# TensorE in program order through three attention pipelines, their side work placed anew

## The chip, the cores and the metric

The kernel runs on one core of a Trainium2 chip. The metric is the time of one launch in microseconds (us) of device time. The kernel before was run three times: 1625.69 to 1627.4 us, median 1627.03 us.

A core has five engines with a queue each: TensorE (PE in the profile, its weight loads PEld), VectorE (DVE), ScalarE (ACT), GpSimd (POOL) and SyncE (SP, which here only starts DMA transfers). TensorE writes its products to PSUM, which has eight banks of 512 f32 columns in 128 partitions.

## The reference, cut to what matters

The model has two blocks. Block 1 has a pooling mixer and a layer of stick-breaking attention; block 2 has latent attention and differential attention, each with modulation (shift, scale, gate) from a vector.

```python
# block 1, layer 1: stick-breaking attention, 16 heads of 64, 512 tokens
logits = q @ k.T * scale                       # strictly causal
a = sigmoid(logits) * prod(sigmoid(-logits) over the later keys)
x = x + (a @ v * silu(z)) @ w_out              # z: gate, a projection of h

# block 2: modulation of each layer, for c and for c_ctx
shift, scale, gate = split(silu(c) @ ada_w[i] + ada_b[i], 3)   # ada_w[i]: 1024 x 3072
h = x * (1 + scale) + shift                    # h_c from the context likewise

# layer 0: latent attention, 16 heads, 512 tokens + 256 of context
q = rope(rms(h W_qa) W_qb);  k, v = rms(h W_kva) W_kvb
o = softmax(q k^T) v * silu(gate)

# layer 1: differential attention, 8 heads, two maps each
o = softmax(q1 k1^T) v - lam * softmax(q2 k2^T) v
o = rms_norm(o) * g_sub * silu(gate)
x = layer_norm(ALPHA * x + gate * (o @ out_w))
```

## The kernel before, in words

Everything is float32. A projection is taken as three products of float32r parts (`mm3`, L147 to L149: high times high, high times low, low times high). Weights come in units of 512 KB through `wraw` (three buffers in SBUF): SP loads them, ACT takes the high part (`wh`, L126), POOL the low part (`wl`, L127).

PSUM is divided into four parts: `lg` (two tiles of two banks, logits), `tr` (two banks, used in turn by all transposes), `pv` (one bank, products of probabilities and values) and `mm` (one bank, for the projections that run inside a pipeline).

Each of the three attentions is a `pipeline` of steps (L238). A step has a first half (logits and what follows on ACT, DVE and POOL) and a second half, emitted `lag` steps later (transposes of the probabilities, products with the values). Into each step *pieces* are emitted: projections for later heads, gates, and the modulation vectors. A piece has a group (a step that needs the group calls `need`, which emits what is left of it) and a due step; in the kernel before, every piece that is due comes between the first and the second half.

- The stick pipeline has 24 steps (8 pairs of heads, three steps each), lag 2. The preparation of a pair transposes its keys and queries into two banks of `tr` (`kT_p`, `qT_p`) and copies them out as high and low parts: keys on ACT and DVE (`K`, L663, L664), queries on ACT (`Q`, L670, L671) and DVE (`QL`, L672). The second half transposes the weights (`aT_p`), copies them out (L713, L715) and multiplies with the values (L725).
- The latent pipeline has 80 steps (16 heads, four blocks of queries and one of the context each), lag 2. The queries of a head are transposed (`qT_p`) and copied out by ACT (L1012) and DVE (L1013). The probabilities are transposed (`PT_p`); after two heads their products with the values go to the one bank of `pv` (L1056), first for the 512 tokens (`PT`), then for the context (`PTc`), and each is multiplied out of the bank by DVE (L1057).
- The differential pipeline has 32 steps (8 heads, four blocks of queries each), lag 1. The preparation of a head (`prep`) transposes queries and keys: `q_p` (four transposes, one bank of `tr`) and `k_p` (four for the first 512 tokens, one bank, and two for the rest, the other bank), in this order, two maps each copied by ACT (L1376, L1377, L1385) and DVE (L1378, L1386). The last second half of a head ends with the products (`pv`, L1418), a norm on ACT and DVE (L1422, L1423, L182 to L187, L1426), four transposes of the normalised output (`o_p`) and their product with the gate (L1431).

The modulation of a layer is a product of a vector pair with 1024 x 3072 weights. `ada_piece` (L755 on) loads one block of 128 rows (`araw`, L764, in a buffer of `wraw`) and adds two products of 32 columns (L767) to a bank of `pv`; eight pieces make one third. The four column groups of 32 of the array hold two halves of the sum and two halves of the columns, so up to four products can run side by side.

What the kernel writes is not the order in which the engines run. The framework's scheduler reorders the instructions of each engine by its own estimates; only what is wrapped in `keep_in_program_order` keeps its place.

Of the kernel before, what the change touches and what calls it, by code (L numbers as in the profile page):

```python
# [19 lines left out]
P = 128  # L20
# [9 lines left out]
FREE = 10 ** 6  # L30
GRID_W = 64
# [10 lines left out]
class Block:  # L42
    def __init__(self, ctx, tc, a, out):
        self.ctx, self.tc, self.nc, self.a, self.out = ctx, tc, tc.nc, a, out
        self.nc.scalar.preload_act_table_set("natural_log_exp_and_others")
        self.st = ""
        self.last_pair = None
# [97 lines left out]
    def mm3(self, out, lh, ll, rh, rl, start, stop):  # L145
        mm = self.nc.tensor.matmul
# [31 lines left out]
    def rsqrt(self, ss, n, scale):  # L178
        """(ss * scale + eps)^-1/2 on a small tile."""
# [25 lines left out]
    def silu_mul(self, out, sg, z):  # L205
        """out = z * sigmoid(z), sg: a tile for the sigmoid."""
# [3 lines left out]
    def split(self, x, pool, tag, gain=None, n=512, bufs=8):  # L210
        """x * gain as the exact sum of two float32r parts."""
# [11 lines left out]
    def row_bcast(self, out, cols):  # L223
        """cols [128 tok, blocks] -> out [128, tok]: the value of each token in every partition."""
        for t in range(cols.shape[1]):
            self.nc.tensor.matmul(out[:, t * P:(t + 1) * P], lhsT=cols[:, t:t + 1].to_broadcast([P, P]), rhs=self.ident, start=True, stop=True)

    def token_ss(self, acc, n, name):
        """acc [128, tok]: sums over partitions, one column for each block of 128 tokens."""
        pr = self.p_tr(name)  # L230
        for t in range(n):
            self.nc.tensor.matmul(pr[:, t:t + 1], lhsT=acc[:, t * P:(t + 1) * P], rhs=self.ones[:, :1], start=True, stop=True)
# [22 lines left out]
    def need(self, group):  # L255
        while any(p[0] <= group for p in self.pieces):
            i = next(i for i, p in enumerate(self.pieces) if p[0] != FREE)
            self.pieces.pop(i)[1]()

# [45 lines left out]
    def pT(self, i, pool):  # L305
        """p[i]^T in two float32r parts."""
# [24 lines left out]
    def ple(self, acts, pT, xT, pool, done, step=None):  # L331
        """x += (p @ ple_w) * sigmoid(x @ ple_gate_w); done(c) follows on each chunk."""
# [164 lines left out]
    def head_norm(self, pp, tb0, dst, pool):  # L497
        """pp [128, 2 blocks, 4 heads x 64] -> dst[:, tb0:tb0+2], each head at unit rms of the normalised input."""
# [27 lines left out]
    def layer1(self):  # L526
# [7 lines left out]
        # k, q and later the outputs of two pairs of heads in each slab  # L534
# [109 lines left out]
    def stick_steps(self, c, ks, qs, vtok, ogs, pool):  # L644
        """Stick-breaking attention of heads 2c and 2c+1: with keep = sigmoid(-l), the weight of key s is
        sigmoid(l_s) times the product of keep over the later keys."""
# [5 lines left out]
        def prep():  # L652
            # [qh; qh], ql and [kh; kl] of each head: two passes carry all three products
# [21 lines left out]
        def first(n, segs):  # L675
# [4 lines left out]
            for e, i, o in segs:  # L680
                w = (i + 1) * P
                s, qi = half[e], slice(i * P, (i + 1) * P)
                nc.tensor.matmul(L[:, o:o + w], lhsT=Q[e][:, qi], rhs=K[e][:, :w], start=True, stop=False)
                nc.tensor.matmul(L[:, o:o + w], lhsT=QL[s, qi], rhs=K[e][s, :w], start=False, stop=False)
                nc.tensor.matmul(L[:, o + i * P:o + w], lhsT=self.identb, rhs=self.maskb, start=False, stop=True)
            kp = pool.tile([P, 1024], F32, tag="sb_k", name="sb_k", bufs=2)
            bt = h["bt", n] = pool.tile([P, 1024], F32, tag="sb_b", name="sb_b", bufs=4)
# [7 lines left out]
            # the last key of a block is masked: its weight is zero as it stands  # L695
# [5 lines left out]
        def second(n, segs):  # L701
# [19 lines left out]
            for j in range(NT):  # L721
                for e in range(2):
                    hd = 2 * c + e
                    av = aT[e][:, 4 * j:10 + j:3, :]
                    nc.tensor.matmul(pv[64 * e:64 * e + 64, j * P:], lhsT=vtok[j][:, hd * 64:(hd + 1) * 64], rhs=av, start=(j == 0), stop=(j == NT - 1))  # L725
# [10 lines left out]
    def ada_setup(self):  # L736
# [9 lines left out]
        # rows 32 * (2 * half of the sum + half of the columns) + vector are summed to 2 * half of the columns + vector  # L746
# [6 lines left out]
    def ada_pieces(self, q, steps):  # L753
        """Shift, scale or gate of a layer (q = 3 * layer + part): one piece for each block of 128 rows."""
        return [(FREE, lambda k=k: self.ada_piece(q, k), n) for k, n in enumerate(steps)]  # L755

    def ada_piece(self, q, k):
        nc = self.nc
        layer, part = divmod(q, 3)
        if k == 0:  # L760
            self.ada_ps = self.p_pv("ada_p")
        ps = self.ada_ps
        raw = self.wp.tile([P, 1024], F32, tag="wraw", name="araw", bufs=3)
        nc.sync.dma_start(out=raw, in_=self.a["ada_w_2"][layer, k * P:(k + 1) * P, part * 1024:(part + 1) * 1024])  # L764
        for b in range(2):
            j = 2 * (k % 2) + b
            nc.tensor.matmul(ps[32 * j:32 * j + 32, :], lhsT=self.cs[:, k, :], rhs=raw[:, b * 512:(b + 1) * 512], start=(k < 2), stop=(k >= 6), tile_position=(0, 32 * j))  # L767
        if k < 7:
            return
        row = self.wp.tile([P, 1024], F32R, tag="wh", name="ada_row", bufs=4).bitcast(F32)  # L770
        nc.vector.tensor_copy(out=row[:, :512], in_=ps)
# [725 lines left out]
```

## Time and profile before

| | |
|---|---|
| runs, median (lowest to highest) | 1627.03 us (1625.69 to 1627.4) |
| profiled execution, span | 1627.5 us |
| PE busy | 1558.4 us, 96% of the span |
| PEld, DVE, ACT, POOL busy | 1260.5, 927.2, 714.9, 601.7 us |
| the three pipelines in the trace | stick 386 to 553 us, latent 779 to 1060 us, differential 1212 to 1573 us |

PE is busy for nearly all of the span. A busy time counts the modelled ends of pipelined matmuls, so it can hide short waits; how far one start lies behind the next says more. A plain f32 matmul (transposes, `ada_p`, `pv` of the latent pipeline) leaves two records where it is done in two passes: for `ada_p` and `pv` the count in a row is twice that of the program's matmuls.

### The profile page before, as it was taken

The numbers are of one execution on the slowest core, as the hardware profiler recorded it, in microseconds if no ns is written. First come the engines' busy times: TensorE is split into PE (matmuls) and PEld (weight loads), VectorE is DVE, ScalarE is ACT, GpSimd is POOL, SyncE is SP. The second block draws the span as 40 slices with busy tenths as digits, with TensorE's granted clock in tenths as the row PEclk, the third lists the DMA queues.
The fourth block names the chain that finished last, engine by engine and source line by source line (L and its number), as shares of the span: only waits on it lengthen the run. The fifth ranks groups of instructions, "written<-read, shape, count | busy, mean of one in ns | idle before, by whom it ended". The sixth has DMA issues, their size and how long they took to land.

```text
span 1627.5 us, 24398 instructions
## 1 busy us (share of the span) xinstructions
PE 1558.4 (96%) x9590; PEld 1260.5 (77%) x9590; DVE 927.2 (57%) x1769; ACT 714.9 (44%) x1315; POOL 601.7 (37%) x431
## 2 busy tenths in 40 slices
PE   6999999999999999999999999997899999999997
PEld 4777889997655688888766666596888888898887
DVE  6676465524766656242655666558855544545566
ACT  5323354436555333332755555623334443544542
POOL 2433555553444453212323332443433323243310
PEclk9999999999999999999999999997997999999999
DMA  5323432322334344311103122254231101121112
GB/s 159 88 78 91 123 117 77 100 92 79 109 124 133 114 133 108 83 46 43 40 2 119 46 71 78 66 182 149 83 96 40 39 27 39 40 66 40 53 64 106
DMA packets 149748, 136.01 MB, mean 84 GB/s; under 512 B 12613, under 2 KB 135225, under 8 KB 149633
## 3 DMA queue, kind: packets, MB, share of 16 engines
q1 hardware_dynamic: 149632, 134.45, 26.6%
q8 instruction: 76, 1.25, 0.3%
q14 instruction: 40, 0.32, 0.1%
HBM read 126.02 MB, written 8.40 MB: 83 GB/s over the span
## 4 chain that ended last, share of the span: by engine, by line
PE 47%; DVE 4%; issue 2%; DMA 2%; ACT 1%; POOL 1%; SPq 0%; DVEq 0%; POOLq 0%; ACTq 0%
PE PT_p L172 5%; PE pv L1056 4%; PE qkv_p L147 3%; PE qkv_p L149 3%; PE qkv_p L148 3%; PE lg L1399 3%; PE pv L1418 3%; PE lg L1398 2%; PE gt_p L147 2%; PE gt_p L148 2%; PE gt_p L149 2%; PE lg L147 2%; PE lg L148 2%; PE lg L149 2%; PE ada_p L767 1%
## 5 line engine op out<-in xcount | busy, mean ns | idle before, releaser
L127 POOL TENSOR_TENSOR wl<-wraw,wh 128x1024 fp32r<-128x1024 f32 (+2 forms) x159 | 376.7, 2379 | 381.2 <-ACT wh L126 362.6
L126 ACT CAST wh<-wraw 128x1024 fp32r<-128x1024 f32 (+2 forms) x164 | 166.6, 1020 | 287.7 <-issue 61.1
L1073 ACT ACTIVATE pe<-lg,st 128x768 f32<-128x768 f32 x160 | 130.4, 816 | 99.3 <-DVE st L1072 76.7
L1072 DVE TENSOR_REDUCE st<-lg 128x1 f32<-128x768 f32 x160 | 134.5, 846 | 47.1 <-PE lg L1399 28.3
L1035 POOL TENSOR_SCALAR pe<-pe,st 128x768 f32<-128x768 f32 (+1 forms) x96 | 73.3, 764 | 159.7 <-DVE st L1074 154.5
L147 PE MATMUL qkv_p<-wh,h 128*128 128x256 f32 x384 | 110.6, 288 | 0.3 <-ACT V L1345 0.2
L149 PE MATMUL qkv_p<-wh,h 128*128 128x256 f32 x384 | 108.9, 284 | 0.2 <-DVE h L217 0.2
L148 PE MATMUL qkv_p<-wl,h 128*128 128x256 f32 x384 | 108.8, 284 | 0.0
L172 PEld LDWEIGHTS PT_p<-ident,pe 128*128 128x128 f32 x640 | 71.6, 142 | 43.5 <-POOL pe L1035 15.9
L172 PE MATMUL PT_p<-ident,pe 128*128 128x128 f32 x640 | 99.3, 280 | 4.4 <-POOL pe L1035 1.4
L1403 POOL TENSOR_SCALAR pe<-pe,st 128x768 f32<-128x768 f32 x32 | 29.1, 909 | 148.1 <-DVE st L1402 96.8
L147 PEld LDWEIGHTS qkv_p<-wh,h 128*128 128x128 f32 x384 | 73.5, 191 | 2.3 <-DVE st L1072 0.5
L147 PE MATMUL out_p<-wh,o 128*128 128x256 f32 x256 | 74.1, 290 | 0.9 <-DVE y L1271 0.8
L148 PE MATMUL out_p<-wl,o 128*128 128x256 f32 x256 | 73.4, 288 | 1.4 <-POOL wl L127 1.4
L147 PE MATMUL kv_p<-wh,kv 128*128 128x256 f32 x256 | 72.7, 284 | 1.3 <-ACT kv L219 1.2
L148 PEld LDWEIGHTS qkv_p<-wl,h 128*128 128x128 f32 x384 | 73.5, 191 | 0.5 <-issue 0.2
L149 PEld LDWEIGHTS qkv_p<-wh,h 128*128 128x128 f32 x384 | 73.2, 191 | 0.8 <-DVE h L217 0.4
L149 PE MATMUL out_p<-wh,o 128*128 128x256 f32 x256 | 73.3, 290 | 0.1
L148 PE MATMUL kv_p<-wl,kv 128*128 128x256 f32 x256 | 72.1, 282 | 0.0
L149 PE MATMUL kv_p<-wh,kv 128*128 128x256 f32 x256 | 71.7, 282 | 0.0
L697 POOL TENSOR_TENSOR sb_b<-sb_b,sb_k 128x1023 f32<-128x1023 f32 (+1 forms) x32 | 43.2, 1360 | 74.3 <-DVE sb_k L694 51.0
L694 DVE TENSOR_TENSOR_SCAN sb_k<-sb_k 128x512 f32<-128x512 f32 (+3 forms) x64 | 56.8, 933 | 6.8 <-ACT sb_k L689 6.5
(453 smaller groups left out, 4574.0 us busy)
## 6 DMA issues: line engine op xcount, KB each, us to landing
araw<-in_ada_w_dram SPq DMA_DIRECT2D x48, 512.0 KB
wraw<-in_diff_w_in_dram SPq DMA_DIRECT2D x32, 512.0 KB
wraw<-in_out_w_dram SPq DMA_DIRECT2D x24, 512.0 KB
wraw<-in_a_w_in_dram SPq DMA_DIRECT2D x16, 512.0 KB
wraw<-in_ple_gate_w_dram SPq DMA_DIRECT2D x16, 512.0 KB
wraw<-in_w_kv_dram SPq DMA_DIRECT2D x16, 512.0 KB
wraw<-in_b_w_in_dram SPq DMA_DIRECT2D x16, 512.0 KB
wraw<-in_mla_w_in_dram SPq DMA_DIRECT2D x11, 512.0 KB
```

The lines of the kernel that those rows point to most:

```text
L126: nc.scalar.copy(h[:, :n], raw[:, :n])
L127: (nc.vector if i < 3 or pool == "ow3" else nc.gpsimd).tensor_tensor(out=l[:, :n], in0=raw[:, :n], in1=h[:, :n].bitcast(F32), op=ALU.subtract)
L147: mm(out, lhsT=lh, rhs=rh, start=start, stop=False)
L148: mm(out, lhsT=lh, rhs=rl, start=False, stop=False)
L149: mm(out, lhsT=ll, rhs=rh, start=False, stop=stop)
L172: self.nc.tensor.transpose(out, in_, self.ident[:in_.shape[0], :in_.shape[0]])
L694: nc.vector.tensor_tensor_scan(out=kp[:, rev], data0=kp[:, rev], data1=kp[:, rev], initial=1.0, op0=ALU.mult, op1=ALU.min)
L1035: nc.gpsimd.tensor_scalar(out=pe, in0=pe, scalar1=st[:, 1:2], scalar2=0.0, op0=ALU.mult, op1=ALU.add)
L1056: nc.tensor.matmul(pv[64 * ee:64 * ee + 64, :], lhsT=V[:, k0 + k, vs], rhs=HH[px][:, k, :], start=(k == 0), stop=(k == nk - 1))
L1072: nc.vector.tensor_reduce(out=st[:, 0:1], in_=L, axis=AX.X, op=ALU.max, negate=True)
L1073: nc.scalar.activation(pe, L, AF.Exp, bias=st[:, 0:1], accum_out=st[:, 2:3])
L1399: nc.tensor.matmul(L[:, cs], lhsT=QL[s, qs], rhs=K[m][s, cs], start=False, stop=True)
```

## The change

1. Inside `pipeline` a flag is set, and while it is set every matmul and transpose is wrapped in `keep_in_program_order`: TensorE then runs them as the program emits them. The other engines are scheduled as before.
2. After a step's first half one due piece is emitted, the other due ones after the second half. `need` leaves modulation pieces and their loads where they are.
3. A modulation piece takes two blocks of rows, loaded by a piece of their own one step earlier; its four products go side by side to the `mm` bank, each complete in itself, and DVE adds them up in an SBUF tile (`arow`). Before, the sum over eight pieces stayed in a bank of `pv`.
4. The pieces of the stick and the latent pipeline get other due steps; those of the differential pipeline keep theirs. One tile of the stick pipeline (`sb_b`) has three buffers where it had four.

```diff
+    def pe(self, ins):
+        return self.tc.keep_in_program_order(ins) if self.in_order else ins
+
+    def mm(self, *args, **kw):
+        return self.pe(self.nc.tensor.matmul(*args, **kw))
+
     def transpose(self, out, in_):
-        self.nc.tensor.transpose(out, in_, self.ident[:in_.shape[0], :in_.shape[0]])
+        self.pe(self.nc.tensor.transpose(out, in_, self.ident[:in_.shape[0], :in_.shape[0]]))
...
         self.mm_banks("mm")
+        self.in_order = True
         for n in range(len(steps) + lag):
             if n < len(steps):
                 steps[n][0]()
-            while pieces and pieces[0][2] <= n:
-                self.piece()
+            self.due(n, 1)
             if n >= lag:
                 steps[n - lag][1]()
-
-    def piece(self):
-        self.pieces.pop(0)[1]()
+            self.due(n, len(pieces))
+        self.in_order = False
+
+    def due(self, n, most):
+        while self.pieces and self.pieces[0][2] <= n and most:
+            p = self.pieces.pop(0)
+            p[1]()
+            most -= p[0] != LOAD
...
-            n = 6 * q + 3
-            pieces += self.ada_pieces(q, [n + k // 2 for k in range(8)])
+            n = 6 * q + 4
+            pieces += self.ada_pieces(q, [n, n + 1, n + 3, n + 4])
...
+    def ada_load(self, q, k):
+        layer, part = divmod(q, 3)
+        raws = self.araw[q, k] = []
+        for i in (2 * k, 2 * k + 1):
+            raws.append(self.wp.tile([P, 1024], F32, tag="wraw", name="araw", bufs=3))
+            self.nc.sync.dma_start(out=raws[-1], in_=self.a["ada_w_2"][layer, i * P:(i + 1) * P, part * 1024:(part + 1) * 1024])
...
-            self.ada_ps = self.p_pv("ada_p")
-        ps = self.ada_ps
-        raw = self.wp.tile([P, 1024], F32, tag="wraw", name="araw", bufs=3)
-        nc.sync.dma_start(out=raw, in_=self.a["ada_w_2"][layer, k * P:(k + 1) * P, part * 1024:(part + 1) * 1024])
-        for b in range(2):
-            j = 2 * (k % 2) + b
-            nc.tensor.matmul(ps[32 * j:32 * j + 32, :], lhsT=self.cs[:, k, :], rhs=raw[:, b * 512:(b + 1) * 512], start=(k < 2), stop=(k >= 6), tile_position=(0, 32 * j))
+            self.arow = self.pools["mla1" if layer else "att"].tile([P, 512], F32, tag="arow", name="arow", bufs=1)
+        row = self.arow
+        ps = self.p_mm("ada_p")
+        for i, raw in enumerate(self.araw.pop((q, k))):
+            for b in range(2):
+                j = 2 * i + b
+                self.mm(ps[32 * j:32 * j + 32, :], lhsT=self.cs[:, 2 * k + i, :], rhs=raw[:, b * 512:(b + 1) * 512], start=True, stop=True, tile_position=(0, 32 * j))
+        if k == 0:
+            nc.vector.tensor_copy(out=row, in_=ps)
+        else:
+            nc.vector.tensor_tensor(out=row, in0=ps, in1=row, op=ALU.add)
...
-            pieces += K(2 * g + 1, n + 2, n + 3)
+            pieces += K(2 * g + 1, n + 1, n + 3)
             if g < 3:
-                pieces += V(g + 1, [n + 6, n + 7, n + 9]) + K(2 * g + 2, n + 10, n + 11) + Q(g + 1, [n + 12, n + 13, n + 14, n + 14, n + 15, n + 16])
+                pieces += K(2 * g + 2, n + 10, n + 11) + Q(g + 1, [n + 12, n + 13, n + 14, n + 14, n + 15, n + 15]) + V(g + 1, [n + 17, n + 18, n + 19])
         for q in range(3, 6):
-            pieces += self.ada_pieces(q, [20 * q - 38 + k for k in range(8)])
+            n = 20 * q - 60
+            pieces += self.ada_pieces(q, [n + 5, n + 7, n + 8, n + 9])
```

The set of TensorE's instructions is the same in both kernels; their order is not. Three places follow, in the order in which TensorE has them.

The end of a head in the differential pipeline, before the change. `qkv_p` is a projection for a later head, `o_p` the transposes behind the norm, `lg` the logits of the next step; the head's last `pv` stands 48 `qkv_p` matmuls ahead of `o_p`:

```order
L147 MATMUL qkv_p<-wh,h_10632 128x256
L148 MATMUL qkv_p<-wl,h_10632 128x256
L149 MATMUL qkv_p<-wh,h_10632 128x256
L172 MATMUL o_p<-ident,on_11751 128x128 x4
L1398 MATMUL lg_11771<-K,Q 128x256
L1399 MATMUL lg_11771<-K,QL 128x256
```

The same place after the change:

```order
L179 MATMUL qkv_p<-wl,h_10668 128x256
L179 MATMUL qkv_p<-wh,h_10668 128x256
L182 MATMUL PT_p<-ident,pe 128x128 x6
L179 MATMUL pv_11762<-V_10789,AT 128x128 x24
L182 MATMUL o_p<-ident,on_11787 128x128 x4
L179 MATMUL lg_11807<-K,Q 128x512
```

The transposes `o_p` now follow the head's last products directly, in seven of the eight heads; in the eighth, products of the out projection stand between.

The preparation of a head in the differential pipeline, before the change, at the last two of the six key transposes (`k_p`); the first four stand 49 rows further up, and `gt_p` is the projection of a gate:

```order
L147 MATMUL gt_p<-h_10730,wh 128x256
L148 MATMUL gt_p<-h_10730,wh 128x256
L149 MATMUL gt_p<-h_10730,wl 128x256
L172 MATMUL k_p<-ident,kr 128x128 x2
L172 MATMUL PT_p<-ident,pe 128x128 x4
L1399 MATMUL lg_12043<-K,QL 128x512
```

The same place after the change:

```order
L179 MATMUL lg_12346<-K,QL 128x256
L182 MATMUL q_p<-ident,qr 128x128 x4
L182 MATMUL k_p<-ident,kr 128x128 x6
L179 MATMUL qkv_p<-wh,hc 128x256
L179 MATMUL qkv_p<-wl,hc 128x256
L179 MATMUL qkv_p<-wh,hc 128x256 x2
```

All ten transposes now stand in one row, through three uses of the two banks of `tr`.

The preparation of a pair of heads in the stick pipeline, before the change (`sb_l` logits, `z_p` the gate's projection, `ada_p` modulation products):

```order
L172 MATMUL kT_p<-ident,ktok 128x128 x4
L172 MATMUL qT_p<-ident,qtok 128x128 x4
L767 MATMUL ada_p<-araw,cs 32x512 x4
L683 MATMUL sb_l<-K_3881,Q_3878 128x256
L684 MATMUL sb_l<-K_3881,QL_3880 128x256
```

The same place of another pair after the change:

```order
L182 MATMUL kT_p<-ident,ktok 128x128 x4
L182 MATMUL qT_p<-ident,qtok 128x128 x4
L179 MATMUL ada_p<-araw,cs 32x512 x4
L182 MATMUL aT_p<-ident,sb_b 128x128 x4
L179 MATMUL pv_3724<-aT,vtok_1840 64x512 x2
L179 MATMUL pv_3724<-aT,vtok_1841 64x384 x2
```

Where logits of older heads and projections stood behind the preparation, the transposes `aT_p` stand now, which take the bank of `kT_p`, and the products that need their copies.

## Rows read from the trace of the kernel before

**Rows 1.** Windows: stretch, PE, PEld, DVE, ACT, POOL busy, granted clock, DMA share, GB/s.

```profile
386.00:553.00 167.00, 160.99 (x841) 96.68 (x841) 113.09 (x169) 93.56 (x131) 74.28 (x49) 1.00 0.34 106
779.00:1060.00 281.00, 276.76 (x1616) 184.16 (x1614) 172.53 (x417) 161.71 (x363) 93.70 (x116) 1.00 0.19 59
1212.00:1573.00 361.00, 358.18 (x2457) 307.20 (x2457) 197.90 (x414) 172.51 (x322) 114.92 (x84) 0.97 0.13 41
```

**Rows 2.** Windows, the modulation products' instructions alone: PE, PEld, DVE busy.

```profile
386.00:553.00 167.00, 19.01 (x96) 2.67 (x96) 2.08 (x3) 1.00 0.34 106
779.00:1060.00 281.00, 25.25 (x96) 3.46 (x96) 2.07 (x3) 1.00 0.19 59
```

**Rows 3.** Timeline, modulation products: start, us, engine, operation, count, [idle before, releaser].

```profile
507.44 1.06 PE L767 MATMUL ada_p<-araw,cs 128*32 128x512 f32 x8
```

**Rows 4.** Timeline, latent pipeline: products of one pair of heads; a later second product.

```profile
1023.02 1.07 PE L1056 MATMUL pv<-PT,V 128*64 128x512 f32 x2
...
1027.06 1.94 PE L1056 MATMUL pv<-PT,V 128*64 128x512 f32 x8
...
1029.30 1.08 PE L1056 MATMUL pv<-PT,V 128*64 128x512 f32 x4
...
1030.67 2.79 PE L1056 MATMUL pv<-PT,V 128*64 128x512 f32 x10
...
1059.25 1.08 PE L1056 MATMUL pv<-PTc,V 128*64 128x256 f32 x8 [0.78 <-DVE og L1057]
```

**Rows 5.** Timeline, stick pipeline: gate projections behind other work and in a run.

```profile
459.16 0.48 PE L148 MATMUL z_p<-b,wh 128*128 128x512 f32 x1
459.48 0.39 PE L149 MATMUL z_p<-b,wl 128*128 128x512 f32 x1
459.71 0.39 PE L147 MATMUL z_p<-b,wh 128*128 128x512 f32 x1
```

**Rows 6.** Timeline, differential pipeline: from a head's last products to `o_p`.

```profile
1571.19 1.50 PE L1418 MATMUL pv<-V,AT 128*128 128x128 f32 x12
...
1575.42 0.69 DVE L1426 TENSOR_TENSOR on<-pv,rs_y 128x512 f32<-128x512 f32 x1
...
1576.26 0.63 PE L172 MATMUL o_p<-ident,on 128*128 128x128 f32 x4 [0.29 <-DVE on L1426]
```

**Rows 7.** Timeline, differential pipeline: the preparation of a head.

```profile
1381.65 0.38 PE L172 MATMUL q_p<-ident,qr 128*128 128x128 f32 x2
1381.87 0.60 PE L172 MATMUL k_p<-ident,kr 128*128 128x128 f32 x4
1382.34 0.58 ACT L1376 CAST Q<-q_p 64x512 fp32r<-64x512 f32 x1
...
1386.30 0.69 DVE L1378 TENSOR_TENSOR QL<-q_p,Q 64x512 fp32r<-64x512 f32 x1 [1.36 <-ACT Q L1377]
```

**Rows 8.** Timeline, latent pipeline: query transposes, and a load of modulation weights.

```profile
1009.68 0.82 PE L172 MATMUL qT_p<-ident,qs 128*96 128x128 f32 x6
1010.95 1.02 DVE L1013 SCALAR_TENSOR_TENSOR qT<-qT_p,qT 96x512 fp32r<-96x512 f32 x2
...
1014.20 0.33 SPq L764 DMA_DIRECT2D araw<-in_ada_w_dram  x1
1018.46 1.05 PE L767 MATMUL ada_p<-araw,cs 128*32 128x512 f32 x4
```

**Rows 9.** Timeline, stick pipeline: key transposes, their last copy, an `aT` copy.

```profile
448.56 0.61 PE L172 MATMUL kT_p<-ident,ktok 128*128 128x128 f32 x4
453.81 0.69 DVE L664 TENSOR_TENSOR K<-kT_p,K 64x512 fp32r<-64x512 f32 x1
...
456.02 0.42 DVE L715 COPY aT<-aT_p 128x256 f32<-128x256 f32 x1 [0.21 <-PE aT_p L172]
```

**Rows 10.** Windows, all engines, around a gap of TensorE outside the pipelines.

```profile
1150.00:1153.50 3.50, 0.36 (x4) 0.16 (x2) 3.50 (x9) 0.00 (x0) 2.82 (x2) 0.99 0.50 159
1153.50:1157.00 3.50, 3.03 (x15) 3.03 (x16) 2.90 (x7) 1.62 (x4) 0.00 (x0) 0.52 0.50 150
```

More of the change, by code (lines that the diff above doesn't have):

```diff
@@ L30 @@
 FREE = 10 ** 6
+LOAD = FREE + 1
 GRID_W = 64
@@ L46, in __init__ @@
         self.st = ""
+        self.in_order = False
+        self.araw = {}
         self.last_pair = None
@@ L145, in mm3 @@
     def mm3(self, out, lh, ll, rh, rl, start, stop):
-        mm = self.nc.tensor.matmul
+        mm = self.mm
         mm(out, lhsT=lh, rhs=rh, start=start, stop=False)
@@ L225, in row_bcast @@
         for t in range(cols.shape[1]):
-            self.nc.tensor.matmul(out[:, t * P:(t + 1) * P], lhsT=cols[:, t:t + 1].to_broadcast([P, P]), rhs=self.ident, start=True, stop=True)
+            self.mm(out[:, t * P:(t + 1) * P], lhsT=cols[:, t:t + 1].to_broadcast([P, P]), rhs=self.ident, start=True, stop=True)
     def token_ss(self, acc, n, name):
@@ L231, in token_ss @@
         for t in range(n):
-            self.nc.tensor.matmul(pr[:, t:t + 1], lhsT=acc[:, t * P:(t + 1) * P], rhs=self.ones[:, :1], start=True, stop=True)
+            self.mm(pr[:, t:t + 1], lhsT=acc[:, t * P:(t + 1) * P], rhs=self.ones[:, :1], start=True, stop=True)
         ss = self.small("tok_ss", n)
@@ L246, in pipeline @@
                 steps[n][0]()
-            while pieces and pieces[0][2] <= n:
-                self.piece()
+            self.due(n, 1)
             if n >= lag:
                 steps[n - lag][1]()
-    def piece(self):
-        self.pieces.pop(0)[1]()
+            self.due(n, len(pieces))
+        self.in_order = False
+    def due(self, n, most):
[3 more added lines that the diff above has]
+            most -= p[0] != LOAD
     def need(self, group):
         while any(p[0] <= group for p in self.pieces):
-            i = next(i for i, p in enumerate(self.pieces) if p[0] != FREE)
+            i = next(i for i, p in enumerate(self.pieces) if p[0] < FREE)
             self.pieces.pop(i)[1]()
@@ L682, in first @@
                 s, qi = half[e], slice(i * P, (i + 1) * P)
-                nc.tensor.matmul(L[:, o:o + w], lhsT=Q[e][:, qi], rhs=K[e][:, :w], start=True, stop=False)
-                nc.tensor.matmul(L[:, o:o + w], lhsT=QL[s, qi], rhs=K[e][s, :w], start=False, stop=False)
-                nc.tensor.matmul(L[:, o + i * P:o + w], lhsT=self.identb, rhs=self.maskb, start=False, stop=True)
+                self.mm(L[:, o:o + w], lhsT=Q[e][:, qi], rhs=K[e][:, :w], start=True, stop=False)
+                self.mm(L[:, o:o + w], lhsT=QL[s, qi], rhs=K[e][s, :w], start=False, stop=False)
+                self.mm(L[:, o + i * P:o + w], lhsT=self.identb, rhs=self.maskb, start=False, stop=True)
             kp = pool.tile([P, 1024], F32, tag="sb_k", name="sb_k", bufs=2)
-            bt = h["bt", n] = pool.tile([P, 1024], F32, tag="sb_b", name="sb_b", bufs=4)
+            bt = h["bt", n] = pool.tile([P, 1024], F32, tag="sb_b", name="sb_b", bufs=3)
             vw = (lambda t: t) if len(segs) == 3 else (lambda t: t.rearrange("p (a b) -> p a b", b=512)[:, :, :256])
@@ L724, in second @@
                     av = aT[e][:, 4 * j:10 + j:3, :]
-                    nc.tensor.matmul(pv[64 * e:64 * e + 64, j * P:], lhsT=vtok[j][:, hd * 64:(hd + 1) * 64], rhs=av, start=(j == 0), stop=(j == NT - 1))
+                    self.mm(pv[64 * e:64 * e + 64, j * P:], lhsT=vtok[j][:, hd * 64:(hd + 1) * 64], rhs=av, start=(j == 0), stop=(j == NT - 1))
             og = ogs[c // 2][:, (c % 2) * 512:(c % 2 + 1) * 512]
@@ L753, in ada_pieces @@
     def ada_pieces(self, q, steps):
-        return [(FREE, lambda k=k: self.ada_piece(q, k), n) for k, n in enumerate(steps)]
+        pieces = []
+        for k, n in enumerate(steps):
+            pieces += [(LOAD, lambda k=k: self.ada_load(q, k), n - 1), (FREE, lambda k=k: self.ada_piece(q, k), n)]
+        return pieces
+    def ada_load(self, q, k):
[4 more added lines that the diff above has]
+            self.nc.sync.dma_start(out=raws[-1], in_=self.a["ada_w_2"][layer, i * P:(i + 1) * P, part * 1024:(part + 1) * 1024])
     def ada_piece(self, q, k):
@@ L784, in ada_piece @@
             pr = self.p_tr("ada_g")
-            nc.tensor.matmul(pr[:4, :], lhsT=self.asel, rhs=row[:, :512], start=True, stop=True)
-            nc.vector.tensor_copy(out=row[:4, 512:], in_=pr[:4, :])
+            self.mm(pr[:4, :], lhsT=self.asel, rhs=row, start=True, stop=True)
+            nc.vector.tensor_copy(out=row[:4], in_=pr[:4, :])
             for b in range(2):
-                nc.sync.dma_start(out=self.gates[layer, :, b], in_=row[2 * b:2 * b + 2, 512:])
+                nc.sync.dma_start(out=self.gates[layer, :, b], in_=row[2 * b:2 * b + 2])
     def gate_rows(self, layer, v, pool):
@@ L1055, in second @@
                         vs = slice((hh - 1 + ee) * 64, (hh + ee) * 64)
-                        nc.tensor.matmul(pv[64 * ee:64 * ee + 64, :], lhsT=V[:, k0 + k, vs], rhs=HH[px][:, k, :], start=(k == 0), stop=(k == nk - 1))
+                        self.mm(pv[64 * ee:64 * ee + 64, :], lhsT=V[:, k0 + k, vs], rhs=HH[px][:, k, :], start=(k == 0), stop=(k == nk - 1))
                 nc.vector.tensor_tensor(out=o, in0=pv, in1=o, op=ALU.mult)
@@ L1397, in first @@
                 for cs in (slice(0, 512), slice(512, 768)):
-                    nc.tensor.matmul(L[:, cs], lhsT=Q[m][:, qs], rhs=K[m][:, cs], start=True, stop=False)
-                    nc.tensor.matmul(L[:, cs], lhsT=QL[s, qs], rhs=K[m][s, cs], start=False, stop=True)
+                    self.mm(L[:, cs], lhsT=Q[m][:, qs], rhs=K[m][:, cs], start=True, stop=False)
+                    self.mm(L[:, cs], lhsT=QL[s, qs], rhs=K[m][s, cs], start=False, stop=True)
                 pes.append(self.soft(L[:, :768], pool, 768, 4))
@@ L1417, in second @@
                 for k in range(6):
-                    nc.tensor.matmul(pv[:, t * P:(t + 1) * P], lhsT=at[:, k, t * P:(t + 1) * P], rhs=V[:, k, j * P:(j + 1) * P], start=(k == 0), stop=(k == 5))
+                    self.mm(pv[:, t * P:(t + 1) * P], lhsT=at[:, k, t * P:(t + 1) * P], rhs=V[:, k, j * P:(j + 1) * P], start=(k == 0), stop=(k == 5))
             sq = on = pool.tile([P, 512], F32, tag="on3", name="on3", bufs=1)
```

6 lines of the change are left out of this document (2 added, 4 removed).

## The prediction

> **What bounds the kernel now.** I read the windows over the three pipelines first, then the timeline of each place at which the change moves work. In the pipelines TensorE is busy for 160.99 of 167, 276.76 of 281 and 358.18 of 361 us [rows 1]: it sets the time, and the 13.0 us of idle time are all that better cover could give back. ACT, DVE and POOL have idle time there (DVE 483.5 busy of 809), so what comes off TensorE comes off the time, and what TensorE waits for is added. The reader is to see two things. The order before is not the program's: whenever a transpose had to wait for a bank or a copy, projections stood ahead of it and covered the wait. The new order takes these covers away at places that the order rows of the change show. In exchange runs of like instructions become longer. So I sum what longer runs save, and what each uncovered wait costs.
>
> **What is saved.** *Modulation products.* They stand in 42 runs before (30 of one product, 8 of two, 4 of four) and in 24 of four after. Their 44.26 us [rows 2] are 1.05 us a run, and four side by side take 1.06 [rows 3], two take 1.05 [rows 8]. Eighteen runs fewer are -19. *Products of the latent pipeline.* One pair of heads has its twelve products in runs that take 1.07, 1.94, 1.08 and 2.79 us, together 6.88 [rows 4]. Two more products side by side cost 0.86 (from x4 to x8), so a run of twelve takes 1.08 + 5 x 0.86 = 5.4; eight pairs save 8 x 1.5 = -12. *Idle time.* -13 at most [rows 1]; I take it whole, since the new waits are counted apart. *Other changes from one kind of product to another.* The order has 261 fewer in the three pipelines, 214 without those just counted. Behind other work a gate projection is followed after 0.32 us, in a run after 0.23 [rows 5], so one change costs up to 0.09, 19 us in all; transposes ahead of logits show almost nothing, and I take -10 (0 to -19). Together -54. The 18 additions on DVE (0.69 us each by the like DVE instruction of [rows 6], 12 us) lie in its idle time: 0, or +12 if its cover were gone.
>
> **What the differential pipeline pays.** *o_p.* Its transposes now follow the head's last products directly. The products ended at 1572.69, DVE's last step of the norm at 1576.11, and `o_p` started at 1576.26 [rows 6]: 3.6 us with ACT and DVE nearly free, and 3.7 from start to start. Nothing can run between, since everything behind `o_p` is kept behind it. Seven heads: +26. With other work on ACT and DVE, by the ratio that `k_p` shows below (4.6 to 2.8), it would be 6.1 each: 26 to 43. *k_p.* The second bank of `k_p` is the bank of `q_p`, which comes free when DVE has made the second low part of the queries. `q_p` ended at 1382.03, DVE at 1386.99 [rows 7]; less the four transposes of `k_p` (0.4) this is 4.6 us uncovered. But ACT did a copy of weights and two of keys in between; bare, four copies of 0.58 and one on DVE of 0.69 with 0.2 of start are 3.2, or 2.8 uncovered. TensorE's stop will take some of this load away, not all, and I take 4.2, nearer to the measured one: seven heads, +29 (20 to 45). In three heads transposes of probabilities follow `k_p` in the other bank and wait once more, 1.3 us each by one copy and its start: +4.
>
> **What the latent pipeline pays.** In 15 heads `PT_p` needs a bank of `qT_p` soon after it. `qT_p` ended at 1010.50, DVE at 1011.97 [rows 8], 1.5 and its start. Eight heads have nothing between, 1.6 each, seven have a short projection, 0.8 each: +18 (10 to 30). The context's products follow the tokens' on the one bank of `pv`; where this was already so, TensorE sat idle for 0.78 us [rows 4], and now seven more pairs do: +6. A load of modulation weights was used 4.3 us after its issue [rows 8], and between the pieces of the last three steps stand only six transposes and six logits products, about 1.7 us, with two of three buffers taken by each piece. Two waits of 2.2 in each of three groups are 13; one load can be ahead, so +8 (0 to 13). Together +32.
>
> **What the stick pipeline pays.** `aT_p` takes the bank of `kT_p` behind `qT_p` and a modulation piece (0.4 + 1.05). `kT_p` ended at 449.17, its last copy at 454.50 [rows 9]: 5.3, or 3.8 uncovered, with activations of other steps ahead of it on ACT. Two copies of each kind bare are some 2.3, or 0.8 uncovered. I take 2.7 at six places, +16 (5 to 23). Behind `aT_p` the products with the values wait for the copies, two of 0.42 and their start [rows 9], eight times 1.0: +8. Together +24.
>
> **The clock.** After a gap of TensorE of 3.1 us the granted clock is 0.52 for 3.5 us, its lower level of 1.2 GHz [rows 10], although TensorE is busy again; half of such a stretch is lost, 1.7. The 14 waits of the differential pipeline are as long as this gap, and shorter ones did mostly nothing of the kind. At 1.5 each: +21 (0 to 24). The Trainium skill's page TensorE: Matmul & The Clock Gate, section HAM oscillation, tells of the same: a kernel that waits between groups of matmuls starts each group on the half clock, for 1.67 us each time. By that figure the term would be an estimated 14 x 0.83 = 12 us and the sum 1701; the stretch in this trace is twice as long, and the sum stands on it.
>
> **The sum.** -19 - 12 - 13 - 10 + 26 + 29 + 4 + 32 + 24 + 21 = +82. The profiled span is 1627.5 us, within 0.5 of the runs' median of 1627.03, so 1710 us.
>
> **The rivals.**
> - *Only the differential pipeline loses.* Its pieces stand where they stood, those of the other two were set anew, and copies that find ACT and DVE idle could come in time there. Then 32 and 24 fall away: 1654 us. Against it: in the order rows of the stick pipeline nothing stands behind the modulation piece, and [rows 4] show the 0.78 with nothing else to do.
> - *The clock stays low longer.* If each of 20 gaps (the 14 and stick's six) cost 3.4 us, the whole of a stretch at the lower level as in [rows 10] once more, 68 instead of 21: 1757 us. For it: a head would have two gaps in some 50 us. Against it: behind the stretch the trace has the full clock again.
> - *Faster: it is the mixing that costs.* TensorE's busy time can hide waits between unlike instructions. If one change of kind costs 0.2 us rather than 0.05, the 214 give back 43, and if ACT and DVE, with TensorE stopped, copy at the bare pace, `k_p` costs 20, the latent pipeline 10 and the stick pipeline 5, with no fall of the clock: -19 - 12 - 13 - 43 + 26 + 20 + 10 + 5 = -26, or 1601 us. It decides from 0.08 a change, if all the waits are that short. Against it: [rows 5] show 0.09 at a place with much mixing, and contended copies at every place above.
> - *No change*, gains and waits alike, 1627 us: it needs waits at the bare pace and the clock kept, without the dear changes of kind.
>
> **How the numbers follow.** All waits as summed: 55%, own range 1680 to 1745. Only the differential pipeline: 20%. Clock low for longer: 11%. Faster by less mixing: 10%. No change: 4%. The lowest bounds of the costs with the highest of the savings are 1627.5 - 63 + 26 + 20 + 4 + 16 + 13 = 1643, and the highest about 1790; with the first two cases and most of the third inside, the range is 1640 to 1775. A measurement of this kernel tells about 0.2% from no change, some 3 us: faster 0.10, same 0.04, slower 0.86.
>
> **What would show it.** In the changed kernel's trace: `ada_p` in 24 runs of 1.05 us; `pv` of the latent pipeline in eight runs of 5.4; TensorE idle ahead of `o_p` for about 3.7 us, released by DVE's last norm step, seven times; idle within `k_p` for 3 to 4.6, released by the second low part of the queries; idle of 1 to 3 ahead of `PT_p` and `aT_p` behind preparations; the granted clock of the differential pipeline well under the 0.97 of before. It would be wrong if TensorE's idle time in the pipelines stayed under some 50 us, if the waits at `o_p` were filled by anything, or if the pace of like matmuls in a row were faster than before by more than the changes of kind counted here.

## The result, and the profile after

The changed kernel takes 1901.53 us (median of four runs, 1898.8 to 1905.06) against 1627.22 us before: a ratio of 1.1693, 95% interval 1.1674 to 1.1712. Forecast were 1710 us and a range of 1640 to 1775 us: the sign was right, the loss is more than three times as large, 274 us for 83.

First the windows over the three pipelines (stretch, busy time of PE, PEld, DVE, ACT and POOL, granted clock, DMA share, GB/s), of the kernel before, cut a little wider than in [rows 1] so that both kernels have the same ends:

```profile
383.00:552.00 169.00, 162.99 (x852) 98.47 (x853) 113.77 (x170) 95.53 (x134) 76.42 (x50) 1.00 0.33 103
778.00:1060.00 282.00, 277.76 (x1625) 185.16 (x1623) 172.81 (x418) 162.69 (x365) 93.98 (x116) 1.00 0.19 59
1205.00:1577.00 372.00, 367.28 (x2531) 315.52 (x2530) 205.88 (x431) 177.60 (x330) 119.83 (x86) 0.97 0.14 42
```

The same windows of the changed kernel:

```profile
382.00:638.00 256.00, 200.33 (x847) 123.59 (x847) 111.63 (x179) 95.06 (x134) 76.11 (x50) 0.79 0.22 68
869.00:1178.00 309.00, 263.90 (x1623) 187.92 (x1623) 175.53 (x427) 162.22 (x368) 93.92 (x116) 0.99 0.16 53
1323.00:1851.00 528.00, 434.23 (x2523) 358.92 (x2521) 206.59 (x430) 179.23 (x329) 117.39 (x86) 0.81 0.10 30
```

The pipelines got 87, 27 and 156 us longer, which is nearly all of it. Two columns tell where: the stretch less PE's busy time is idle time, and the busy time times what the clock lacks of 1.00 is an estimate of what the lower clock took (the clock column is a mean over the whole stretch, idle time included).

| us | stick | latent | differential | sum |
|---|---|---|---|---|
| longer | 87 | 27 | 156 | 270 |
| idle time of TensorE, more by | 49.7 | 40.9 | 89.1 | 180 |
| taken by the lower clock, more by (busy x (1 - clock)) | 42 | 3 | 72 | 117 |
| left: work saved | -5 | -17 | -5 | -27 |

The view of waits of the changed kernel, TensorE's part (us in total, times, longest) says whom it waited for:

```profile
PE k_p L182 <- DVE QL L1410: 41.4, 8, 6.1
PE aT_p L182 <- DVE K L681: 28.6, 7, 4.6
PE o_p L182 <- DVE on L1458: 25.3, 8, 3.6
PE aT_p L182 <- DVE aT L732: 18.0, 24, 1.7
PE PT_p L182 <- DVE qT L1045: 12.4, 14, 1.3
...
PE qkv_p L179 <- DVE og L847: 10.4, 3, 3.5
PE pv L179 <- DVE og L1089: 6.3, 8, 0.8
...
PE ada_t L179 <- DVE arow L800: 4.9, 3, 1.6
```

Five of these lines are waits that the prediction names. The three others are `aT_p` behind a copy of its own bank (18.0), a projection that waits for a gate to leave the one bank of the projections (10.4), and, in the stick pipeline, the products that follow a finished third of the modulation (`ada_t`) and wait for DVE's last addition (4.9).

One head of the differential pipeline, the timeline (start, us, engine, operation, idle before and releaser) at its preparation, which answers [rows 7]:

```profile
1434.13 0.60 PE L182 MATMUL q_p<-ident,qr 128*128 128x128 f32 x4
1434.57 0.60 PE L182 MATMUL k_p<-ident,kr 128*128 128x128 f32 x4
...
1435.16 0.59 ACT L209 ACTIVATE og<-gt_p 128x512 f32<-128x512 f32 x1
1435.65 0.56 ACT L1408 CAST Q<-q_p 64x512 fp32r<-64x512 f32 x1
1436.11 0.63 ACT L210 ACTIVATE og<-og 128x512 f32<-128x512 f32 x1
...
1440.45 0.69 DVE L1410 TENSOR_TENSOR QL<-q_p,Q 64x512 fp32r<-64x512 f32 x1
...
1441.29 0.66 PE L182 MATMUL k_p<-ident,kr 128*128 128x128 f32 x2 [6.13 <-DVE QL L1410]
```

ACT works off the activations of the gate that was computed just before, between the copies of the queries. And the windows that follow this wait, and those around the wait at `o_p` of the same head (1468.8 to 1472.4):

```profile
1435.30:1441.20 5.90, 0.00 (x0) 0.00 (x0) 3.46 (x6) 5.39 (x10) 2.34 (x1) 0.78 0.27 90
1441.20:1449.00 7.80, 6.88 (x16) 3.62 (x16) 2.89 (x5) 2.31 (x5) 0.00 (x0) 0.50 0.00 0
1449.00:1459.10 10.10, 10.10 (x33) 7.33 (x33) 5.29 (x12) 3.46 (x7) 1.81 (x2) 0.50 0.01 2
...
1468.80:1472.40 3.60, 0.04 (x1) 0.03 (x1) 2.03 (x6) 1.01 (x3) 0.00 (x0) 1.00 0.00 0
1472.40:1475.80 3.40, 3.40 (x9) 1.89 (x9) 1.12 (x2) 0.00 (x0) 0.00 (x0) 0.54 0.00 0
1475.80:1482.90 7.10, 7.10 (x28) 5.97 (x28) 2.96 (x6) 1.98 (x4) 0.91 (x1) 0.50 0.01 2
1482.90:1489.80 6.90, 6.90 (x44) 5.43 (x44) 1.74 (x3) 1.92 (x4) 0.00 (x0) 1.00 0.00 0
```

A wait of 3.6 us is followed by 10.5 us of work at 0.50 to 0.54, one of 6 us by 18 us. In [rows 10] it was 3.5 us after a gap of 3.1. In this head, what follows the wait of 6 us costs more than the wait: half of the 18 us is 9. It is one of the three heads with the longest wait at `k_p`. In the next head projections follow `k_p`, not transposes and logits, and a wait of 5.2 us is followed by only 4.4 us at 0.50:

```profile
1490.40:1495.60 5.20, 0.03 (x2) 0.04 (x1) 3.59 (x8) 3.99 (x8) 0.91 (x1) 0.77 0.00 0
1495.60:1500.00 4.40, 4.40 (x21) 4.40 (x22) 1.41 (x3) 0.73 (x2) 0.00 (x0) 0.50 0.00 0
```

Over the whole pipeline the waits cost more than the clock, 89 us against 72. The kernel before has such a stretch too, inside its own differential pipeline: 17 us with TensorE busy throughout, among logits and projections, and 2 us before it a wait of only 1.3:

```profile
1218.40:1219.70 1.30, 0.00 (x0) 0.00 (x0) 1.30 (x3) 1.02 (x3) 0.00 (x0) 1.00 0.00 0
1219.70:1221.70 2.00, 1.98 (x6) 0.99 (x6) 1.15 (x6) 0.85 (x2) 0.91 (x1) 1.00 0.00 0
1221.70:1238.80 17.10, 17.10 (x55) 12.25 (x55) 10.20 (x19) 7.82 (x15) 3.88 (x4) 0.50 0.00 0
```

In the latent pipeline the steps came as forecast, the products of a pair of heads in one run of 5.4 us and the second product 0.8 behind it, at the full clock:

```profile
970.13 0.74 PE L182 MATMUL PT_p<-ident,pe 128*128 128x128 f32 x4 [1.28 <-DVE qT L1045]
...
990.70 5.37 PE L179 MATMUL pv<-PT,V 128*64 128x512 f32 x24
996.86 1.08 PE L179 MATMUL pv<-PTc,V 128*64 128x256 f32 x8 [0.80 <-DVE og L1089]
```

### The profile page after: what moved, and what is told of

Same layout as the page of the kernel before. It is cut to its first block, busy times and chain, and to the rows that moved or that the text cites. A ratio compares the mean times of both kernels' runs of the same rounds, so it can differ in the third digit from the quotient of the medians.

```text
span 1902.2 us, 24480 instructions
## 1 busy us (share of the span) xinstructions
PE 1654.7 (87%) x9590; PEld 1338.4 (70%) x9590; DVE 927.0 (49%) x1787; ACT 715.6 (38%) x1315; POOL 599.6 (32%) x431
## 4 chain that ended last, share of the span: by engine, by line
PE 42%; DVE 8%; ACT 5%; issue 2%; POOL 1%; DMA 1%; DVEq 0%; SPq 0%; POOLq 0%; ACTq 0%
PE qkv_p L179 10%; PE lg L179 9%; PE gt_p L179 6%; PE pv L179 5%; PE out_p L179 5%; PE PT_p L182 3%; DVE st L1104 2%; ACT pe L1105 2%; PE qb_p L179 1%; DMA araw<-in_ada_w_dram 1%; POOL pe L1067 1%; PE ada_p L179 0%; DVE qT L1045 0%; DVE QL L1410 0%; DVE h L227 0%
## 5 line engine op out<-in xcount | busy, mean ns | idle before, releaser
L179 PE MATMUL qkv_p<-wh,h 128*128 128x256 f32 x768 | 162.4, 309 | 10.8 <-DVE og L847 10.4
L179 PEld LDWEIGHTS qkv_p<-wh,h 128*128 128x128 f32 x768 | 136.7, 216 | 14.6 <-issue 12.9
L182 PE MATMUL PT_p<-ident,pe 128*128 128x128 f32 x640 | 100.4, 291 | 24.2 <-DVE qT L1045 12.4
L179 PE MATMUL out_p<-wh,o 128*128 128x256 f32 x512 | 100.4, 296 | 2.4 <-DVE o L227 0.9
L179 PE MATMUL lg<-kTs,qT 96*128 96x512 f32 (+1 forms) x480 | 100.0, 344 | 0.5 <-ACT qT L1044 0.5
L179 PE MATMUL kv_p<-wh,kv 128*128 128x256 f32 x512 | 92.7, 283 | 1.3 <-ACT kv L229 1.2
L179 PEld LDWEIGHTS out_p<-wh,o 128*128 128x128 f32 x512 | 84.6, 202 | 4.1 <-DVE o L227 1.5
L179 PEld LDWEIGHTS lg<-kTs,qT 96*128 96x128 f32 x480 | 77.2, 192 | 13.4 <-issue 2.7
L179 PEld LDWEIGHTS qkv_p<-wl,h 128*128 128x128 f32 x384 | 83.0, 216 | 0.1
L179 PEld LDWEIGHTS kv_p<-wh,kv 128*128 128x128 f32 x512 | 79.5, 191 | 2.3 <-ACT kv L229 1.4
L179 PE MATMUL ple_a<-x,wh 128*128 128x512 f32 x256 | 81.1, 393 | 0.0
```

The costliest lines, as they stand in the source:

```text
L179: return self.pe(self.nc.tensor.matmul(*args, **kw))
L182: self.pe(self.nc.tensor.transpose(out, in_, self.ident[:in_.shape[0], :in_.shape[0]]))
```

## The experiments

The theory after the result: program order uncovers waits of TensorE (180 us), and the lower clock that follows them takes another 117. The rivals: the pieces' new places, or the modulation products' new way, cost it; and for the clock, that something other than the waits pulls it down.

**Program order, taken away (e1_free_all).** In `pipeline`:

```diff
-        self.in_order = True
+        self.in_order = False
```

> The changed kernel with TensorE free to be reordered everywhere; the pieces' new places and the side-by-side modulation products stay. Theory of waits (program order uncovers waits of TensorE, and the half clock follows these waits): the idle time of 195 us and the low clock in the three pipelines of the changed kernel go, what is left is near the kernel before: 1605 to 1640 us. Rival, the new places and the modulation products through SBUF cost most of it: over 1700 us.

1647.08 us, ratio 1.0131 (1.0103 to 1.0159). Its three windows:

```profile
383.00:569.00 186.00, 171.28 (x842) 102.67 (x843) 126.81 (x179) 95.18 (x132) 79.05 (x50) 0.97 0.31 94
796.00:1079.00 283.00, 275.06 (x1623) 186.10 (x1621) 176.38 (x427) 162.98 (x366) 94.17 (x116) 0.99 0.18 58
1224.00:1594.00 370.00, 365.07 (x2526) 313.34 (x2525) 207.67 (x431) 177.57 (x329) 120.59 (x86) 0.98 0.14 42
```

Program order thus costs 70 us in the stick pipeline, 26 in the latent and 158 in the differential, 254 of the 274. But 7 us over the upper end of the expectation stay, in the stick pipeline (186 us for 169): something else in the change costs about 17 us.

**Program order in two pipelines (e3_free_diff).**

```diff
-        self.in_order = True
+        self.in_order = len(steps) != 32
```

> The changed kernel with TensorE free to be reordered in the differential pipeline only. The changed kernel's trace has 157 us more there than before (89 idle, some 73 of half clock, little saved). Theory of waits: 1902 - 157 = 1745 us, 1730 to 1765. Rival, pieces and their places: these are the same in this pipeline, so no more than 30 us go, 1870 us or more.

1740.23 us in one run, as expected: the differential pipeline takes 370 us at a clock of 0.98, and the other two stay at 256 and 307. The losses add up pipeline by pipeline.

**The pieces back in their places (e2_old_places).**

```diff
-            self.due(n, 1)
+            self.due(n, len(pieces))
...
-            pieces += K(2 * g + 1, n + 1, n + 3)
+            pieces += K(2 * g + 1, n + 2, n + 3)
```

and likewise the steps of `V`, of the last `Q` and of the modulation pieces.

> The changed kernel with the pieces at the steps and between the halves where the kernel before had them (modulation pieces of two row blocks at the steps of their second block or near), TensorE in program order. Theory of waits: program order is what costs, so this is as slow as the changed kernel or slower, 1880 to 2000 us. Rival, the new places cost it: under 1780 us.

1926.25 us in one run: 25 us slower than the changed kernel, so the new places take away some of what program order costs; they are not its cause.

**The waits filled with useless products (e4_fill, e9_fill_long, e10_fill_short).** These leave every wait in place and give TensorE something to do in it. The first, in the differential pipeline (`fill` writes so many products, of 0.12 us each at the full clock, to a PSUM bank that nobody reads then):

```diff
+                if t0 and h:
+                    self.fill(self.chain[h - 1], 36)
                 pr = self.p_tr("k3_p")[:, :n * P]
...
+            self.fill(H, 30)
             pr = self.p_tr("o3_p")
```

> The changed kernel with useless products added on TensorE in the two waits of each head of the differential pipeline: 30 (3.5 us at the full clock) ahead of o_p, 36 (4.2 us) between the fourth and fifth k_p, 15 places in all; their result is read by nobody. Theory: the granted clock falls because TensorE stands idle there, so filling the waits keeps it up, and adding work makes the kernel faster by most of the 84 us lost at the half clock there: 1830 to 1865 us. Rival, the clock falls for another reason (the kind of work, a long wait elsewhere): 1895 to 1915 us. Second rival, the added products delay what follows: over 1915 us.

1877.91 us: faster by 24 with 492 products more, though not by as much as expected. The window of its differential pipeline:

```profile
1317.00:1822.00 505.00, 455.57 (x2985) 394.11 (x2986) 206.77 (x431) 179.28 (x329) 116.87 (x86) 0.90 0.10 31
```

Idle time fell from 94 to 49 us (in three heads the filling itself waited for the bank of the projections), and what the clock takes from 82 to 46; against these 81 us stand 58 of products (492 of 0.12 us, an estimate). So the clock comes back when the waits are filled, and half of the waits is half of the loss. The other two do it in the stick pipeline, once in its six long waits, once in the short ones between the transposes `aT_p`:

```diff
             aT, bt = h["aT"], h["bt", n]
+            if n == 2 and c < 6:
+                self.fill(h["after"], 34)
```

> The changed kernel, program order kept, with 34 useless products (4.0 us at the full clock) on TensorE in the six long waits of the stick pipeline, ahead of the aT_p that follows a preparation; they are read by nobody. The stick pipeline has 256 us, 56 idle, 109 at the half clock. If the long waits (4.2 us each) pull the clock down, the low clock falls to a third or less and the kernel gets faster in spite of the added work: 1865 to 1890 us. If the many short waits (31 of 0.3 to 2 us) hold it down, it stays and the added products cost what they run beyond the waits at the half clock: 1900 to 1925 us.

```diff
+                if e != segs[0][0] or i != segs[0][1]:
+                    self.fill(h if n < 2 else h.get("after", h), 6)
                 for j in range(i + 1):
                     self.transpose(pr[:, (b0 + j) * P:(b0 + j + 1) * P], bt[:, o + j * P:o + (j + 1) * P])
```

> The changed kernel with 6 useless products (0.7 us at the full clock) ahead of each later group of aT_p transposes of the stick pipeline, 40 places, 28 us of added work, where the waits are short (0.76 us on average, 25 of them). If the long waits pull the clock down, it stays low and the kernel is slower by the work beyond the waits: 1905 to 1930 us. If the short ones do, the low clock in the stick pipeline goes below 50 us: 1870 to 1895 us.

1890.03 and 1891.63 us, one run each, against 1898.8 to 1905.06 of the changed kernel. The window of the stick pipeline with the long waits filled, and then with the short ones:

```profile
378.00:625.00 247.00, 209.54 (x1047) 139.78 (x1049) 110.50 (x179) 93.46 (x132) 74.73 (x50) 0.88 0.24 71
```

```profile
379.00:628.00 249.00, 209.75 (x1082) 147.82 (x1084) 111.20 (x179) 94.20 (x133) 75.13 (x50) 0.86 0.23 71
```

Neither either-or held: the clock rises from 0.79 to 0.88 by the one and to 0.86 by the other, which leaves about 60 and 70 us at the half clock of 109, where a third and less than 50 were expected. Long waits and short ones both hold it down here. The latent pipeline, with 45 us of short waits and none above 2.1 us, keeps 0.99: short waits alone, spread over 309 us, did it no harm. What makes the difference between the two pipelines isn't shown.

**Cover by real work, program order kept (e5_cover_diff, e8_cover_stick).** The first emits `o_p` and the last two `k_p` one step later, behind logits and a piece:

```diff
+            late, self.late = self.late, []
             if n < len(steps):
                 steps[n][0]()
             self.due(n, 1)
+            for f in late:
+                f()
...
+            if h:
+                self.late.append(lambda: keys(4, 2))
...
+            self.late.append(tail)
```

> The changed kernel, program order kept, but in the differential pipeline the transposes o_p and the last two k_p of a head are emitted one step later, behind the logits and the first piece of that step. Theory of waits: the cover is what is missing; of the 94 us idle there some 25 to 35 stay (three heads have only logits as cover, other waits are untouched) and most of the 84 us lost at the half clock goes: 1765 to 1810 us. Rival, the copies on ACT and DVE are too slow in program order and the waits come back at the next place: over 1850 us.

1839.89 us: 62 us are back, 30 short of the least expected, and the rival's 1850 isn't reached either. The wait at `k_p` went, and in three heads the next user of the bank has it, by the same releaser:

```profile
1425.85 1.51 PE L183 MATMUL PT_p<-ident,pe 128*128 128x128 f32 x6 [6.13 <-DVE QL L1417]
...
1431.93 0.69 PE L183 MATMUL k_p<-ident,kr 128*128 128x128 f32 x2
```

That is 18.4 of the 41.4 us at `k_p`. Other waits of `PT_p`, for a copy by ACT, grew from 2.3 to 13.8, and of the 25.3 us at `o_p` 4.0 are left, as the view of waits of this pipeline has it:

```profile
PE PT_p L183 <- DVE QL L1417: 18.4, 3, 6.1
PE PT_p L183 <- ACT AT L1128: 13.8, 11, 2.4
...
PE o_p L183 <- DVE on L1470: 4.0, 2, 3.6
```

The second puts logits and a modulation piece between `qT_p` and the next `aT_p` of the stick pipeline:

```diff
             if n == 1 and "next" in h:
-                h["next"]()
+                self.late.append(h["next"])
```

with `late` emptied at the end of a step.

> The changed kernel, program order kept, but in the stick pipeline the transposes kT_p and qT_p of the next pair are emitted at the end of their step, so that logits and a modulation piece stand between them and the next aT_p. Theory of waits: the 25 us ahead of aT_p (4.2 at six places) fall by 10 to 18 and the low clock there (109 of 256 us) with them by a quarter to a half: 1865 to 1890 us. Rival, the copies come later by as much and K is late for its logits instead: 1895 to 1915 us.

1907.92 us in one run, no gain. The waits of `aT_p` behind `K` fell from 28.6 to 8.5 us, but those behind a copy of `aT` rose from 18.0 to 30.7, and `ada_t` now waits 5.0 for `K`; the clock of the stick pipeline is 0.75. The rival had the time right and the place wrong: the logits wait no longer than before. With two banks that all transposes use in turn, program order can hand a late copy on to whoever comes next.

**The rest of 17 us in the stick pipeline.** Three runs: the lost buffer of `sb_b` alone, on the kernel before (e6_before_sb3); no program order and the old places (e7_free_old); and this with the modulation products in the bank of `pv` again, still summed in SBUF (e13_free_pv):

```diff
-            bt = h["bt", n] = pool.tile([P, 1024], F32, tag="sb_b", name="sb_b", bufs=4)
+            bt = h["bt", n] = pool.tile([P, 1024], F32, tag="sb_b", name="sb_b", bufs=3)
```

> The kernel before with one edit: sb_b of the stick pipeline has three buffers where it had four. The changed kernel without program order took 1.3% more than the kernel before, nearly all of it in the stick pipeline (+17 us). If the lost buffer is why, 1638 to 1650 us. If the new places or the modulation products through the mm bank are why, 1623 to 1632 us.

> TensorE free to be reordered, the pieces at the steps of the kernel before, the modulation products four side by side through SBUF, sb_b with three buffers. If the new places cost the 1.3%, this is 1608 to 1628 us, since the products save up to 18 us. If the lost buffer or the way of the modulation products costs it, it stays at 1638 to 1655 us.

```diff
-        ps = self.p_mm("ada_p")
+        ps = self.p_pv("ada_p")
```

> As the run with TensorE free, the old places and the products summed in SBUF (1645.6 us), but the four products go to the bank of pv and not to the bank of the projections. If sharing the one bank of the projections is what cost 18 us there (mostly in the stick pipeline, where a gate's projection holds it for 5 us and more), 1615 to 1630 us. If the additions on DVE and the tile in SBUF cost it, 1638 to 1650 us.

The buffer costs nothing in the kernel before: 1627.31 us, ratio 1.0005 (0.999 to 1.0019). With the old places it stays at 1645.61 us, 1.0117 (1.0092 to 1.0141), so the places aren't it. The other bank brings it to 1633.76 us, 1.0055 (1.0034 to 1.0076), a little above what was expected. So 10 to 12 of the 18 us come from sharing the one bank of the projections (in the profiled executions the stick pipeline takes 194 us with the products in the bank of the projections and 180 with them in that of `pv`), and 6 to 9 stay open, for the sum in SBUF and the pairs of loads.

**A version that might beat both (e12_before_four_kept).** The kernel before, with two blocks of rows in a modulation piece and only their four products kept in order:

```diff
+        for i, raw in enumerate(raws):
+            for b in range(2):
+                j = 2 * i + b
+                self.tc.keep_in_program_order(nc.tensor.matmul(ps[32 * j:32 * j + 32, :], lhsT=self.cs[:, 2 * k + i, :], rhs=raw[:, b * 512:(b + 1) * 512], start=(k == 0), stop=(k == 3), tile_position=(0, 32 * j)))
```

> The kernel before with the modulation pieces of two row blocks each, their four products emitted together and kept in program order, still summed in the bank of pv; nothing else kept in order. 33 runs of these products instead of 42, which by 1.05 us a run saves 9 us: 1614 to 1624 us. Rival, the two loads at once make the products wait, or the kept products hold up others: 1628 to 1640 us.

1623.61 us, ratio 0.9993 (0.9978 to 1.0008): no difference that can be told. It lies inside the expected range only because the kernel before took 1625.29 us beside it. The products do come in 33 runs, and TensorE's time for them falls from 44.3 to 37.6 us, but the kernel's time doesn't follow; why is not shown. No run beat the kernel before.

## Why the prediction was wrong, step by step

The forecast missed by 192 us. Of these, 96 are the clock's, 80 the waits' and 14 the savings', all in the three pipelines.

- **What bounds the kernel, and that covers are lost: right.** TensorE sets the time, and the waits stand at the places named, by the releasers named: `o_p` 25.3 us for 26, `PT_p` behind `qT` 12.4 for 18, the latent pipeline's `pv` 6.3 for 6, its loads of modulation weights 3.0 for 8.
- **The savings: right in kind, a third too high.** The runs came as forecast (`pv` 5.37 for 5.4, `ada_p` in 24 runs). The table leaves -27 for -41. Without program order the side-by-side products save nothing: the modulation products still take 43 us, against 44.26 [rows 2], since the scheduler parts them again. (The 42 runs before are 4 of one product, 30 of two and 8 of four; the prediction's split doesn't add up to the 96 products, but its sum uses only the 42.)
- **Waits: too low by 80 us.** Summed were 115 us; idle are 195 in the three pipelines (180 more than before). The waits that the prediction names came to 120, in part by luck: `k_p` and `aT_p` behind `K` took 70 us for 45, the others 50 for 70. `k_p` was taken at 4.2, between the bare pace and the one measured, in the hope that a stopped TensorE would leave ACT and DVE freer; it is 5.2 on average. Where it is 6.1, the activations of a gate come just then; where it is 5.2, those of the logits. The 8 us for products behind the copies of `aT` were 1.1. The 75 us that are over stand at places that the prediction doesn't name: 18.0 for `aT_p` behind a copy of its own bank, 10.4 for the bank of the projections, 4.9 for additions, the rest in many small waits.
- **The clock: the step that failed.** It was priced at 14 waits of 1.5 us, 21 in all, from a gap outside the pipelines [rows 10], and the stick pipeline at nothing, because short gaps had "mostly" done nothing. It took about 117. A stretch at 1.2 GHz behind a wait lasts 4.4, 10 and 18 us in the heads shown, and not 3.5, and in the stick pipeline waits of 0.3 to 2 us keep it low together with the long ones. The kernel before had the sign: its clock of 0.97 in the differential pipeline [rows 1] is mostly the stretch of 17 us shown above, five times as long as the one that the price was taken from, and behind a short wait. The rival that had the clock low for longer, at 68 us, was still too small. That waits cause it is shown, for those that were filled, by the three runs in which useless work raised the clock and made the kernel faster. The Trainium skill's page TensorE: Matmul & The Clock Gate, section HAM oscillation, has the mechanism; its 1.67 us for each gap are far from what these stretches measure, and the measurement decides.
- **The modulation products' new way.** It was costed by its additions on DVE, at nothing. In the stick pipeline `ada_t` waits 4.9 us for them, and the bank that the products share with the projections costs 10 to 12 us where TensorE is free to be reordered. What it costs in program order was not measured.

What stays open: how the 117 us divide between long and short waits, as they act together; what makes one wait cost 4.4 us at the half clock and another 18 (the length of the wait and the work behind it both differ); and the 6 to 9 us of the sum in SBUF and the pairs of loads.

## What to carry to other kernels

An order that looks idle-free on the busiest engine is worth more than the sum of the waits it hides: price each uncovered wait of TensorE with the work that runs at the half clock behind it, here 4 to 18 us behind waits of 3.6 to 6, and read that length inside the pipeline itself. Before fixing an order by hand, follow each shared bank to the copy that frees it, and put real work of at least that length between; moving one user away can hand the wait to the next (18.4 of 41.4 us at `k_p`). Products packed side by side save TensorE time only as long as nothing parts them, and a bank that other work needs takes some of it back.

## What the runs showed of the hardware that was not expected

- After a wait of TensorE of 3.6 us the clock stood at 1.2 GHz for 10 us in which TensorE was busy throughout, after one of 6 us for 18 us, and after one of 5.2 us, with projections behind it, for 4.4. In the kernel before it stood there for 17 us shortly behind a wait of 1.3.
- Useless products in the waits made the kernel faster: 24 us with 492 of them in the differential pipeline, 11 with 204 and 10 with 240 in the stick pipeline.
- Waits of up to 2.1 us, 45 us of them in 309, left the clock at 0.99 in one pipeline, and others of that length, 27 us in 256 beside seven longer ones, went with 0.79.
